# A one-layer mLSTM, attention and expert-lookup kernel: gathered rows consumed later, DRAM fetches moved forward, one more PSUM bank for U

## The chip, the cores and the metric

The kernel runs on one core of a Trainium2 chip. The metric is the device time of the core in microseconds (us), the median of three runs. Below, PE is the tensor engine (PEld its weight loads), DVE the vector engine, ACT the scalar engine, POOL the general-purpose engine, and SP the engine that here only issues DMAs. Every engine executes its own instructions in the order in which the program has them; semaphores tie engines to each other.

## What is computed

One layer over 512 tokens of width 2048, all in float32: a mixer of two branches (a chunked mLSTM and a causal attention with forget gates), a cross attention to 256 memory rows, and a lookup feed-forward, each followed by a residual and a layer norm. The feed-forward is where most of the change lies:

```python
q = (x @ w_pq).reshape(B, S, PEER_HEADS, 2, PEER_DK // 2)
sc = jnp.einsum('bshpd,hpnd->bshpn', q, sub_keys)
top_s, top_i = lax.top_k(sc, PEER_TOPK)
...
g = jax.nn.softmax(best_s, -1)
...
u = expert_u[it]                                   # 128 rows of 2048 for each token
a = jnp.einsum('tkd,td->tk', u, xt)
hact = jax.nn.gelu(a, approximate=False) * gt
return jnp.einsum('tk,tkd->td', hact, expert_v[it])
```

Each token picks 128 of 16384 experts (8 heads, 16 each), takes the dot product of the token with each expert's row of U, a gelu times the gate, and the sum of the experts' rows of V with these weights.

## The kernel before

**Weights.** Every large product is made from two float32r parts of each operand (high and low), so a product is three matmuls: high by high, high by low, low by high. A weight tile of 128 x 1024 comes by DMA into `raw` (L148, on SP's queue), ACT casts it to `whi` (L134), and DVE subtracts to get `wlo` (L137). In the first half every eighth such subtraction is made by POOL instead (L136, `SHARE`). The rings that hold these tiles are small: two to six `whi` and `wlo` in all.

**Token blocks.** Block A is the first 128 tokens, block B the other 384. A runs ahead through the whole mixer and the top-k, so that its experts are known while B still computes. In order, the stages are: A's path and the memory's projections, with B's mLSTM heads woven in; the end of B's heads (`run(heads)`, L1043); B's branch product (`branch_ml`, whose left operand is the tiles H, written to DRAM by the heads and loaded back, one tile pair to a weight load); B's attention (`fox`), its merge, output product, norm, cross attention, norm; B's top-k. Small pieces of attention and norm are "ridden" between weight loads (`mid`, `ride`, L166 to L179).

**Two ways through the experts.** Blocks A (128 tokens) and 96 further tokens (64 and 32) take the gathered way, `gathered` (L851). For each of its 128 choices (for fewer tokens, the 128 partitions hold several choices of one token at once), POOL issues an indirect DMA that puts one row of U per partition into `rows` (L846; 128 x 2048, three buffers), and DVE multiplies it with the token's own row `xacc` and sums (L860). Then the same is done for V, with a multiply-add into `xacc` (L873). The function is a generator: each `next` requests one row tile and emits the work on it. `load_w` calls it at a fixed rate while B computes (258 steps to 315 weight loads for block A). A gather carries a dependency on the newest weight split (`after(i, last())`), which keeps the requests from running ahead.

The other 288 tokens take the dense way: all 128 x 128 experts are gone through by first key. For first key `c`, `stage_a(c)` makes U's product (16 slices of the width by 3 parts, 48 matmuls into one PSUM bank `pa`, of which there are two), ACT applies the gelu into `ga` (L1223) and the result goes to DRAM (`gad`). Meanwhile the gates are built as one-hot products (L1182 to L1195) and written to DRAM (`gd`). `stage_h(c)` fetches both back (`G` for four keys at a time, `gb` for one, both on SP's queue, L1232 and L1236), multiplies them on DVE (L1240) and splits the product into `hph` and `hpl`. `stage_o` multiplies these with V: blocks of J = 8 keys, and for each block four quarters `q` of the width, four weight loads each. `stage_h` is called for the block's keys as quarter 0 comes to them. U runs LOOK = 68 keys ahead of V, so 68 keys are done before V starts, and the rest is interleaved with V by `fill`. Of the gathers' 194 steps for the 96 tokens, EARLY = 44 are taken in the first part and the rest in V; in V they are tied to the newest split of `stage_h` (`cur[0] = paced[c]`).

**Order.** Within an engine, the order of instructions is not that of the source: a scheduler places them by a timeline that it simulates, under the dependencies, the buffers of each pool and the manual dependencies of `after`.

Of the kernel before, what the change touches and what calls it, by code (L numbers as in the profile page):

```python
# [10 lines left out]
F32 = mybir.dt.float32  # L11
# [5 lines left out]
ALU = mybir.AluOpType  # L17
# [29 lines left out]
def build(tc, I, out):  # L47
    nc = tc.nc
    with ExitStack() as ctx:
# [461 lines left out]
        def fox(R, fp, ft, hold):  # L511
# [3 lines left out]
            def keys(qd):  # L515
                def ev(s, b, ks=quads[qd]["k"]):
                    ks[s] = ft(n)
                    nc.vector.tensor_copy(ks[s], b[:, :n])  # L518
# [331 lines left out]

        def gathered(t, r0, n, i, last):  # L851

# [4 lines left out]
            dots = gat.tile([P, P], F32, tag="dots", bufs=2, name=nm("dots"))  # L857
            for k in range(n):
                rows = gather_rows("peer_u", ei, k, last)
                nc.vector.scalar_tensor_tensor(rows, rows, 1.0, xacc, op0=ALU.mult, op1=ALU.mult,  # L860
                                               accum_out=dots[:, k:k + 1])
                yield True

            al = gat.tile([P, 1], F32, tag="al", bufs=1, name=nm("al"))
            if n < P:
                nc.vector.memset(al, 0.0)
            nc.vector.memset(al[:n], ALPHA)
            nc.scalar.mul(xacc, xacc, al)
            nc.scalar.activation(dots[:, :n], dots[:, :n], AF.Gelu)
            nc.vector.tensor_mul(dots[:, :n], dots[:, :n], gg[:, :n])  # L870
            for k in range(n):
                rows = gather_rows("peer_v", ei, k, last)
                nc.vector.scalar_tensor_tensor(xacc, rows, dots[:, k:k + 1], xacc, op0=ALU.mult, op1=ALU.add)  # L873
                yield True
            if n < P:
# [175 lines left out]
        with tc.tile_pool(name="hb", bufs=1, reuse_waits="tile") as hp:  # L1051
            HB = []
# [103 lines left out]

        def a_bank():
            return BK["pool"].tile([P, 512], F32, tag="s2", bufs=2, name=nm("pa"))

        def o_bank(i=0):  # L1160
# [41 lines left out]

        LOOK = 68
        EARLY = 44
        GA_N = 3
        J = 8
        gas, hs, paced, gates = {}, {}, {}, [None]
# [20 lines left out]

        def stage_h(c):
            if c % 4 == 0:  # L1230
                gt = mn.tile([P, NDENSE // GB, 4, GB], F32, tag="G", bufs=2, name=nm("G"))
                nc.sync.dma_start(gt, gd[:, :, c:c + 4])  # L1232
                gates[0] = gt
            if c in spilled:
                ga = mn.tile([P, NDENSE], F32, tag="gb", bufs=2, name=nm("gb"))
                nc.sync.dma_start(ga, gad[c])  # L1236
            else:
                ga = gas.pop(c)
            gv = ga.rearrange("p (b t) -> p b t", t=GB)
            nc.vector.tensor_mul(gv, gv, gates[0][:, :, c % 4])  # L1240
# [4 lines left out]
        cur = [None]  # L1245
        jobs = chain(*(gathered(TB - 1, r0, n, 1 + i, lambda: cur[0]) for i, (r0, n) in enumerate(GATHERED)))
        NT = -(-NDENSE // P)
        lwd, xr = [], {}

        def stage_o(c0, q, fill):  # L1250
# [3 lines left out]
            for m in range(J // 2):  # L1254
                vh, vl, _ = load_pair(I["vq"][c0 // 2 + m, q])
                todo = []
                for j in range(2):
                    c = c0 + 2 * m + j
                    if q == 0:
                        stage_h(c)  # L1260
                        cur[0] = paced[c]
                    a, b = hs[c]
                    for s in range(4):
                        sl = slice(j * 512 + s * P, j * 512 + (s + 1) * P)
                        todo.append((banks[s][:, :NDENSE], vh[:, sl], vl[:, sl], a, b, c, True))
                products(todo, c0, c0 + J - 1)
                fill(q * (J // 2) + m)
            if last and q == 0:
# [27 lines left out]
        for a in range(ahead[0]):  # L1296
            stage_a(a)
            cur[0] = work["last"]
            while done * LOOK < a * EARLY:
# [91 lines left out]
```

## Time and profile before

| | |
|---|---|
| time, median of 3 runs | 5062.73 us (5058.62 to 5063.53) |
| time of the profiled execution | 5072.05 us |
| its span | 5070.3 us |
| DMA moved | 1420.97 MB, mean 280 GB/s |
| mean granted PE clock | 0.977 |
| gathers (L846) | 224 of U, 224 of V |
| multiply on a row of U (L860) | 2336 ns each, DVE |
| multiply-add on a row of V (L873) | 2399 ns each, DVE |
| high part of a weight tile (L134) | 1051 ns each, ACT |
| low part of a weight tile (L137) | 1271 ns each, DVE |
| low part on POOL (L136) | 2579 ns each |

Engine times are busy times. A row of a view that ends in `[3.44 <-DVE c L518]` says that the engine stood idle for 3.44 us before this instruction and that what it waited for was DVE's write of the tile `c` in line 518. A row of waits reads: the waiting engine, tile and line, what it waited for, and then the total in us, how often, and the longest. Matmuls are pipelined, so the duration of one is longer than the distance to the next. The chain of waits that ended last runs along PE through the products of V and U, then through the last norm, which POOL and DVE finish.

### The profile page before, as it was taken

The page shows a single profiled execution, that of the slowest core. Times are in us where ns is not written, and L with a number is a line of the kernel's source. Part 1 is how long each engine was busy: PE and PEld are TensorE (multiplying, and loading weights), DVE is VectorE, ACT ScalarE, POOL GpSimd, SP SyncE. Part 2 cuts the span into 40 slices and gives each one's busy share as a digit, 9 for nine tenths or more (in the row PEclk, how much of TensorE's full clock was granted, in tenths as well). Part 3 has the DMA queues.
Part 4 walks back from the last instruction along what each step waited for, and adds up shares of the span by engine and source line. Part 5 has one row for each costly group of instructions (what it writes and reads, how often), then busy time and mean ns, then how long its engine had stood idle before and what let it go on. Part 6 is the DMA issues. An engine that isn't in the chain of part 4 may idle for free. (4 is left out here: it accounts for less than half of the span.)

```text
span 5070.3 us, 74427 instructions
## 1 busy us (share of the span) xinstructions
PE 4789.3 (94%) x28401; PEld 4397.2 (87%) x28401; DVE 3728.7 (74%) x5387; ACT 2122.9 (42%) x3046; POOL 1270.4 (25%) x1039
## 2 busy tenths in 40 slices
PE   7999999999989999998899999999989999999997
PEld 6888777777779999887888879999989999999987
DVE  6676767666977777666776565898878788787875
ACT  6556666565423233333224324434444333433332
POOL 1122223121324433323332221321001222121210
PEclk8999999999999999999999999999999999999998
DMA  7788878777689988777885774677769889898983
GB/s 247 254 283 284 279 261 276 264 249 234 225 310 357 351 326 305 275 257 260 293 323 212 258 254 162 211 256 259 281 248 364 328 336 344 328 354 321 358 302 123
DMA packets 375415, 1420.97 MB, mean 280 GB/s; under 512 B 43341, under 2 KB 104397, under 8 KB 316017
## 3 DMA queue, kind: packets, MB, share of 16 engines
q1 hardware_dynamic: 263904, 827.14, 47.3%
q0 software_dynamic: 89408, 551.06, 28.7%
q10 hardware_dynamic: 21744, 38.02, 2.0%
q8 instruction: 222, 3.64, 0.3%
q14 instruction: 137, 1.11, 0.1%
HBM read 1343.32 MB, written 72.62 MB: 279 GB/s over the span
## 5 line engine op out<-in xcount | busy, mean ns | idle before, releaser
L134 ACT CAST whi<-raw 128x1024 fp32r<-128x1024 f32 x1472 | 1533.0, 1051 | 2145.8 <-PE mm L205 823.3
L137 DVE TENSOR_TENSOR wlo<-raw,whi 128x1024 fp32r<-128x1024 f32 x1352 | 1703.7, 1271 | 698.8 <-ACT whi L134 504.6
L873 DVE SCALAR_TENSOR_TENSOR xacc<-rows,dots,xacc 128x2048 f32<-128x2048 f32 x224 | 537.3, 2399 | 220.6 <-DMA rows<-in_peer_v,eid 218.8
L860 DVE SCALAR_TENSOR_TENSOR rows<-rows,xacc 128x2048 f32<-128x2048 f32 x224 | 522.9, 2336 | 97.7 <-DMA rows<-in_peer_u,eid 97.6
L846 POOL DMA_INDIRECT rows<-in_peer_v,eid x224 | 336.0, 1500 | 1010.8 <-DVE wlo L137 389.5
L205 PE MATMUL pa<-Ch,whi 128*128 128x288 f32 x2048 | 564.8, 300 | 14.4 <-ACT ga L1223 13.0
L846 POOL DMA_INDIRECT rows<-in_peer_u,eid x224 | 309.6, 1382 | 1037.1 <-DVE rows L860 320.4
L205 PE MATMUL po<-hph,whi 128*128 128x288 f32 x2048 | 533.6, 298 | 32.6 <-ACT hph L134 27.3
L205 PE MATMUL pa<-Cl,whi 128*128 128x288 f32 x2048 | 562.8, 299 | 0.0
L205 PE MATMUL po<-hpl,whi 128*128 128x288 f32 x2048 | 533.1, 297 | 6.1 <-DVE hpl L137 6.1
L136 POOL TENSOR_TENSOR wlo<-raw,whi 128x1024 fp32r<-128x1024 f32 x120 | 309.5, 2579 | 723.8 <-ACT whi L134 444.4
L205 PE MATMUL mm<-xh,whi 128*128 128x384 f32 x1280 | 441.3, 347 | 9.1 <-DVE c L518 5.9
L205 PE MATMUL mm<-xl,whi 128*128 128x384 f32 x1280 | 433.9, 340 | 0.0
L205 PEld LDWEIGHTS po<-hph,whi 128*128 128x128 f32 x2048 | 374.8, 190 | 39.6 <-ACT hph L134 30.6
L205 PEld LDWEIGHTS pa<-Ch,whi 128*128 128x128 f32 x2048 | 389.8, 190 | 18.3 <-ACT ga L1223 14.8
L205 PEld LDWEIGHTS pa<-Cl,whi 128*128 128x128 f32 x2048 | 389.9, 190 | 1.7 <-issue 1.7
L205 PEld LDWEIGHTS po<-hpl,whi 128*128 128x128 f32 x2048 | 375.3, 190 | 7.4 <-DVE hpl L137 7.4
L205 PE MATMUL po<-hph,wlo 128*128 128x288 f32 x2048 | 349.5, 298 | 6.0 <-DVE wlo L137 6.0
L205 PE MATMUL pa<-Ch,wlo 128*128 128x288 f32 x2048 | 323.0, 297 | 3.7 <-DVE wlo L137 3.7
L205 PEld LDWEIGHTS po<-hph,wlo 128*128 128x128 f32 x2048 | 301.5, 191 | 6.5 <-DVE wlo L137 6.5
L205 PEld LDWEIGHTS pa<-Ch,wlo 128*128 128x128 f32 x2048 | 289.8, 189 | 4.7 <-DVE wlo L137 3.9
L205 PE MATMUL mm<-xh,wlo 128*128 128x384 f32 x1280 | 258.5, 337 | 5.3 <-DVE wlo L137 5.3
(440 smaller groups left out, 8778.6 us busy)
## 6 DMA issues: line engine op xcount, KB each, us to landing
raw<-in_w_in SPq DMA_DIRECT2D x512, 512.0 KB
raw<-in_uT SPq DMA_DIRECT2D x256, 512.0 KB
raw<-in_vq SPq DMA_DIRECT2D x256, 512.0 KB
raw<-in_w_xkv SPq DMA_DIRECT2D x64, 512.0 KB
raw<-in_w_br_ml SPq DMA_DIRECT2D x64, 512.0 KB
raw<-in_w_br_fx SPq DMA_DIRECT2D x64, 512.0 KB
raw<-in_w_out SPq DMA_DIRECT2D x64, 512.0 KB
raw<-in_w_xq SPq DMA_DIRECT2D x64, 512.0 KB
```

Of the source, the lines that this page charges most:

```text
L134: nc.scalar.copy(hi, src)
L136: return nc.gpsimd.tensor_sub(lo, src, hi.bitcast(F32))
L137: return nc.vector.tensor_sub(lo, src, hi.bitcast(F32))
L205: nc.tensor.matmul(o, w if stat else x, x if stat else w, start=k == first and x is xh and not part, stop=k == last and part == 1)
L846: i = nc.gpsimd.indirect_dma_start(out=rows, out_offset=None, in_=I[table], in_offset=bass.IndirectOffsetOnAxis(ap=ei[:, k:k + 1], axis=0))
L860: nc.vector.scalar_tensor_tensor(rows, rows, 1.0, xacc, op0=ALU.mult, op1=ALU.mult, accum_out=dots[:, k:k + 1])
L873: nc.vector.scalar_tensor_tensor(xacc, rows, dots[:, k:k + 1], xacc, op0=ALU.mult, op1=ALU.add)
```

## The change

- `gathered` requests a row tile and keeps it; the multiply on it is emitted `lag` steps later: two for block A, one for the other 96 tokens. The multiply now has a dependency on the newest weight split too (before, only the gather had one). The requests for V start while the last rows of U are still held.
- In V, "the newest split" is that of the last loaded weight tile of V or U, no longer that of `stage_h`.
- `fetch(c)` is taken out of `stage_h`. A call for key `c` also fetches `c+1` and `c+2` if these come from DRAM; `gb` has four buffers instead of two.
- In quarter 3 of a block, `stage_h` is called for the keys of the next block, two after each weight load.
- `stage_a` takes its bank from `sm_bank`, which goes round three banks, two of which are those that it had.
- LOOK is 72 instead of 68.
- The first 8 weight loads of B's branch are emitted before the rest of B's heads is settled and their pools are closed; its `sg` tiles get a pool of their own. H is loaded two tile pairs to a weight load.
- `keys` in the attention copies its tiles out of PSUM on ACT instead of DVE.

```diff
             def keys(qd):
                 def ev(s, b, ks=quads[qd]["k"]):
                     ks[s] = ft(n)
-                    nc.vector.tensor_copy(ks[s], b[:, :n])
+                    nc.scalar.copy(ks[s], b[:, :n])
...
-        def gathered(t, r0, n, i, last):
+        def gathered(t, r0, n, i, last, lag):
...
-            for k in range(n):
-                rows = gather_rows("peer_u", ei, k, last)
-                nc.vector.scalar_tensor_tensor(rows, rows, 1.0, xacc, op0=ALU.mult, op1=ALU.mult,
-                                               accum_out=dots[:, k:k + 1])
+            held = []
+
+            def use():
+                s, rows = held.pop(0)
+                k = s % n
+                if s == n:
...
+                    nc.scalar.mul(xacc, xacc, al)
+                    nc.scalar.activation(dots[:, :n], dots[:, :n], AF.Gelu)
+                    nc.vector.tensor_mul(dots[:, :n], dots[:, :n], gg[:, :n])
+                if s < n:
+                    after(nc.vector.scalar_tensor_tensor(rows, rows, 1.0, xacc, op0=ALU.mult, op1=ALU.mult,
+                                                         accum_out=dots[:, k:k + 1]), last())
+                else:
+                    after(nc.vector.scalar_tensor_tensor(xacc, rows, dots[:, k:k + 1], xacc,
+                                                         op0=ALU.mult, op1=ALU.add), last())
+
+            for s in range(2 * n):
+                if len(held) == lag:
+                    use()
+                held.append((s, gather_rows("peer_v" if s >= n else "peer_u", ei, s % n, last)))
                 yield True
...
-            for k in range(n):
-                rows = gather_rows("peer_v", ei, k, last)
-                nc.vector.scalar_tensor_tensor(xacc, rows, dots[:, k:k + 1], xacc, op0=ALU.mult, op1=ALU.add)
-                yield True
+            while held:
+                use()
...
-        work.update(jobs=gathered(0, 0, P, 0, lambda: work["last"]), rate=258 / 315)
+        work.update(jobs=gathered(0, 0, P, 0, lambda: work["last"], 2), rate=258 / 315)
         run(heads)
+        sgp = ctx.enter_context(ExitStack())
+        sg = sgp.enter_context(tc.tile_pool(name="sg", bufs=1, side="right", reuse_waits="tile"))
+        HB = []
+        branch = branch_ml(B, HB, lambda: sg.tile([P, B.n], F32, tag="sg", bufs=9, name=nm("sg")))
+        for _ in range(8):
+            next(branch)
         settle()
...
-            mid(*[load_h] * 16)
-            run(branch_ml(B, HB, lambda: hp.tile([P, B.n], F32, tag="sg", bufs=9, name=nm("sg"))))
+            mid(*[lambda: (load_h(), load_h())] * 8)
+            run(branch)
+        sgp.close()
...
-        LOOK = 68
+        LOOK = 72
...
-            bank = a_bank()[:, :NDENSE]
+            bank = sm_bank()[:, :NDENSE]
...
-        def stage_h(c):
+        fetched = {}
+
+        def fetch(c):
+
             if c % 4 == 0:
                 gt = mn.tile([P, NDENSE // GB, 4, GB], F32, tag="G", bufs=2, name=nm("G"))
                 nc.sync.dma_start(gt, gd[:, :, c:c + 4])
                 gates[0] = gt
             if c in spilled:
-                ga = mn.tile([P, NDENSE], F32, tag="gb", bufs=2, name=nm("gb"))
+                ga = mn.tile([P, NDENSE], F32, tag="gb", bufs=4, name=nm("gb"))
                 nc.sync.dma_start(ga, gad[c])
             else:
                 ga = gas.pop(c)
+            fetched[c] = ga, gates[0]
+
+        def stage_h(c):
+            for f in range(c, min(c + 3, NC_)):
+                if f in fetched:
+                    continue
+                if f != c and f not in spilled:
+                    break
+                fetch(f)
+            ga, gt = fetched[c]
...
-            paced[c] = split(a, b, ga)
+            split(a, b, ga)
...
-        jobs = chain(*(gathered(TB - 1, r0, n, 1 + i, lambda: cur[0]) for i, (r0, n) in enumerate(GATHERED)))
+        jobs = chain(*(gathered(TB - 1, r0, n, 1 + i, lambda: work["last"], 1) for i, (r0, n) in enumerate(GATHERED)))
...
-                vh, vl, _ = load_pair(I["vq"][c0 // 2 + m, q])
+                vh, vl, work["last"] = load_pair(I["vq"][c0 // 2 + m, q])
...
-                    if q == 0:
+                    if c not in hs:
                         stage_h(c)
-                        cur[0] = paced[c]
...
                 products(todo, c0, c0 + J - 1)
+                if q == 3 and not last:
+                    for c in (c0 + J + 2 * m, c0 + J + 2 * m + 1):
+                        stage_h(c)
                 fill(q * (J // 2) + m)
```

More of the change, by code (lines that the diff above doesn't have):

```diff
@@ L857, in gathered @@
             dots = gat.tile([P, P], F32, tag="dots", bufs=2, name=nm("dots"))
-            for k in range(n):
-                rows = gather_rows("peer_u", ei, k, last)
-                nc.vector.scalar_tensor_tensor(rows, rows, 1.0, xacc, op0=ALU.mult, op1=ALU.mult,
-                                               accum_out=dots[:, k:k + 1])
-                yield True
[L864 to L870, printed above, removed]
-            for k in range(n):
-                rows = gather_rows("peer_v", ei, k, last)
-                nc.vector.scalar_tensor_tensor(xacc, rows, dots[:, k:k + 1], xacc, op0=ALU.mult, op1=ALU.add)
-                yield True
+            held = []
[3 more added lines that the diff above has]
+                if s == n:
+                    al = gat.tile([P, 1], F32, tag="al", bufs=1, name=nm("al"))
+                    if n < P:
+                        nc.vector.memset(al, 0.0)
+                    nc.vector.memset(al[:n], ALPHA)
+                    nc.scalar.mul(xacc, xacc, al)
[11 more added lines that the diff above has]
+                held.append((s, gather_rows("peer_v" if s >= n else "peer_u", ei, s % n, last)))
+                yield True
+            while held:
+                use()
             if n < P:
@@ L1051, in build @@
         with tc.tile_pool(name="hb", bufs=1, reuse_waits="tile") as hp:
-            HB = []
             def load_h():
@@ L1155, in build @@
         work["share"] = 0
-        def a_bank():
-            return BK["pool"].tile([P, 512], F32, tag="s2", bufs=2, name=nm("pa"))
         def o_bank(i=0):
@@ L1206, in build @@
         J = 8
-        gas, hs, paced, gates = {}, {}, {}, [None]
+        gas, hs, gates = {}, {}, [None]
         rings[:] = [W, E]
         def stage_a(c):
-            bank = a_bank()[:, :NDENSE]
+            bank = sm_bank()[:, :NDENSE]
             for kt in range(2):
@@ L1238, in stage_h @@
                 ga = gas.pop(c)
+            fetched[c] = ga, gates[0]
[7 more added lines that the diff above has]
+            ga, gt = fetched[c]
             gv = ga.rearrange("p (b t) -> p b t", t=GB)
-            nc.vector.tensor_mul(gv, gv, gates[0][:, :, c % 4])
+            nc.vector.tensor_mul(gv, gv, gt[:, :, c % 4])
             a, b = pair(mn, "hp", [P, NDENSE], 2 * J + 2)
-            paced[c] = split(a, b, ga)
+            split(a, b, ga)
             hs[c] = (a, b)
-        cur = [None]
-        jobs = chain(*(gathered(TB - 1, r0, n, 1 + i, lambda: cur[0]) for i, (r0, n) in enumerate(GATHERED)))
+        jobs = chain(*(gathered(TB - 1, r0, n, 1 + i, lambda: work["last"], 1) for i, (r0, n) in enumerate(GATHERED)))
         NT = -(-NDENSE // P)
@@ L1297, in build @@
             stage_a(a)
-            cur[0] = work["last"]
             while done * LOOK < a * EARLY:
```

## The prediction

> **What bounds the kernel now.** I read the page's totals first, then a table of stretches, then who waits for whom inside the stretches that the change touches, and last single rows of the timeline. The profiled execution has a span of 5070.3 us and a time of 5072.05 us; the median of the runs is 5062.73. Terms below are in the profiled execution's own time, and I take the sum off the median, 9.3 us lower.
>
> ```profile
> span 5070.3 us, 74427 instructions
> ...
> PE 4789.3 (94%) x28401; PEld 4397.2 (87%) x28401; DVE 3728.7 (74%) x5387; ACT 2122.9 (42%) x3046; POOL 1270.4 (25%) x1039
> ```
>
> The tensor engine (PE) sets the end: it is busy 94% of the span, and no other engine is over 74%. No matmul is added or removed, so the change can only win what PE loses. Where it loses, the table of stretches shows (start:end, length, then busy time of PE, PEld, DVE, ACT, POOL, granted clock, share of the DMA engines, GB/s):
>
> ```profile
> 0.00:1300.00 1300.00, 1231.41 (x5977) 1013.50 (x5978) 908.78 (x1375) 782.83 (x1068) 296.37 (x286) 0.98 0.78 263
> ...
> 1400.00:1500.00 100.00, 82.88 (x389) 70.77 (x388) 75.72 (x108) 29.10 (x41) 30.25 (x25) 0.91 0.82 303
> 1500.00:2050.00 550.00, 548.64 (x3085) 529.38 (x3085) 408.73 (x475) 175.32 (x233) 214.48 (x162) 1.00 0.90 334
> 2050.00:2450.00 400.00, 353.09 (x1823) 320.64 (x1822) 251.45 (x281) 117.08 (x190) 122.85 (x102) 0.95 0.73 259
> 2450.00:3050.00 600.00, 571.63 (x2803) 502.39 (x2802) 400.07 (x400) 190.53 (x260) 186.63 (x163) 0.98 0.73 267
> ...
> 3250.00:3750.00 500.00, 471.25 (x3514) 466.19 (x3513) 439.17 (x922) 205.76 (x435) 90.51 (x66) 0.98 0.76 272
> 3750.00:3800.00 50.00, 30.57 (x202) 28.50 (x201) 29.67 (x76) 15.63 (x59) 1.70 (x2) 0.83 0.61 226
> 3800.00:4900.00 1100.00, 1080.01 (x8017) 1069.23 (x8016) 892.32 (x981) 430.26 (x529) 232.54 (x157) 0.99 0.92 343
> 4900.00:5000.00 100.00, 88.19 (x614) 83.74 (x614) 55.76 (x82) 36.24 (x46) 4.50 (x5) 0.93 0.61 201
> ```
>
> Idle PE time is length less busy time: 17.1 us where block B's heads give way to its branch (1400:1500), 46.9 in the attention and merge of B (2050:2450), 28.8 where top-k, U and the gates are built (3250:3750), 19.4 at the start of V (3750:3800), 20.0 over all of V (3800:4900) and 11.8 at its last block (4900:5000). The clock falls in the same stretches, so some of the busy time there is slow as well. These two rows of one form (4 matmuls of 384 columns) say how: after an idle 1.49 us they took 0.97 us, after 3.12 us they took 1.65.
>
> ```profile
> 2396.75 0.97 PE L205 MATMUL mm<-Ah,whi 128*128 128x384 f32 x4 [1.49 <-ACT Ah L141]
> ...
> 2440.26 1.65 PE L205 MATMUL mm<-Al,whi 128*128 128x384 f32 x4 [3.12 <-DVE Al L142]
> ```
>
> **Gathered rows used two steps later (A).** DVE runs in order, and today it stands still until a gathered row has landed. Total waits of DVE for rows, in 1400:1500, 1500:2050, 2050:2450 and 2450:3050:
>
> ```profile
> DVE rows L860 <- DMA rows<-in_peer_u,eid: 11.8, 6, 5.4
> ...
> DVE rows L860 <- DMA rows<-in_peer_u,eid: 44.5, 22, 4.2
> ...
> DVE xacc L873 <- DMA rows<-in_peer_v,eid: 116.4, 34, 8.5
> ...
> DVE xacc L873 <- DMA rows<-in_peer_v,eid: 90.0, 34, 7.7
> ```
>
> Such a wait reaches PE like this: DVE loses 3.69 us on a row, multiplies it for 2.35, only then copies four key tiles out of PSUM, and PE has stood 3.44 us for that copy.
>
> ```profile
> 2201.41 2.35 DVE L873 SCALAR_TENSOR_TENSOR xacc<-rows,dots,xacc 128x2048 f32<-128x2048 f32 x1 [3.69 <-DMA rows<-in_peer_v,eid]
> ...
> 2203.74 1.94 DVE L518 COPY c<-mm 128x384 f32<-128x384 f32 x4
> ...
> 2204.35 0.44 PE L205 MATMUL mm<-xh,whi 128*128 128x384 f32 x1 [3.44 <-DVE c L518]
> ```
>
> How long does a row take? Counted from the first of each, these are the 127th gather and the 127th multiply: 7.6 us from issue to use, with DVE waiting.
>
> ```profile
> 2034.19 1.00 POOL L846 DMA_INDIRECT rows<-in_peer_u,eid  x1 [0.76 <-DVE wlo L137]
> ...
> 2041.79 2.29 DVE L860 SCALAR_TENSOR_TENSOR rows<-rows,xacc 128x2048 f32<-128x2048 f32 x1 [3.00 <-DMA rows<-in_peer_u,eid]
> ```
>
> A step comes every 315/258 weight loads. A load carries 24 matmuls of 0.178 us (550 us by 3085), 4.3 us, so a step is 5.2 us and two steps 10.4: longer than 7.6. The built order of both programs agrees. In the stretch 2050:2450 (gathers 128 to 184) there lie 0 or 1 weight splits of DVE between the split that a gather waits for and its multiply in 37 of 51 cases before, 2 or more in 49 of 57 after. So I expect nearly all of the 116.4 us to go. What PE gets of it is bounded by PE's own waits in 2050:2450:
>
> ```profile
> PE mm L205 <- DVE Al L142: 11.6, 6, 3.6
> PE sm L590 <- DVE fst L576: 8.7, 2, 5.0
> ...
> PE mm L205 <- DVE c L518: 5.9, 2, 3.4
> PE sm L590 <- DVE fpt L597: 5.8, 2, 5.1
> PE mm L205 <- DVE wlo L137: 2.9, 3, 1.6
> PE mm L205 <- POOL wlo L136: 2.5, 1, 2.5
> ```
>
> Without the key copies those behind DVE are 11.6+8.7+5.8+2.9 = 29.0. I take two thirds, 19, since 0:1300, which the change leaves almost alone, has 5.3% idle anyway, and that much of 400 us (21) should remain here. In 2450:3050 idle is 4.7%, below that floor: 0, though DVE waits 90 us there.
>
> **Key copies on ACT (L518).** Sixteen copies for B, 0.49 us each in the row above, and sixteen small ones for A. ACT is busy 117 of 400 us, and other evictions of that shape sit on it already; DVE loses 8 us of work. The 5.9 us of PE waits bound the gain; 0 is the other end if ACT has them late instead. I take 4.
>
> The clock in 2050:2450 costs at most 0.05 of 353 us, 18; in proportion to idle time won (23 of 46.9) that is 9. Sum of the stretch: 19+4+9 = 32, between 8 and 60. [...]
>
> **Eight loads of the branch moved ahead of the heads' end.** Waits of PE in 1400:1500:
>
> ```profile
> PE sm L488 <- DVE st L480: 6.7, 1, 6.7
> PE mm L205 <- DVE wlo L137: 5.3, 3, 2.4
> PE sm L488 <- DVE o L483: 4.2, 2, 2.4
> ```
>
> In the built order the 12 transposes of the last head (L488), which stood in one row, now have some 170 branch matmuls between and ahead of them: the DVE chain of the norm (6.7+4.2) gets cover. The wlo waits lie beside row waits (11.8); I take half. The clock costs at most 0.09 of 83 us, 7.5; I take 6. Against it: the H tiles are now loaded two to a weight load over 8 loads instead of one over 16. A load then moves 0.52 MB of weights, 0.39 of H and 0.82 rows of 1.05 MB, 1.77 MB in 4.3 us, or 412 GB/s. At the 334 GB/s of 1500:2050 it takes 5.3 us, 8 us late over eight loads; at no cost if the raw buffers carry it. I take 3. Sum 10.9+2.6+6-3 = 16, between 0 and 24.
>
> **U in three banks, LOOK 72.** In 3250:3750 PE waits for the bank that the gelu empties:
>
> ```profile
> PE pa L205 <- ACT ga L1223: 13.0, 8, 3.3
> ...
> PE pa L205 <- DVE wlo L137: 3.7, 1, 3.7
> ```
>
> A third bank gives each gelu one more key (48 matmuls, 6.5 us at 0.135, 1080 us by 8017) of patience, against a longest wait of 3.3; I take 9 of 13.0, as the bank is shared with the scores. From wlo 3, from the clock (0.02 of 471) 4: 16, between 3 and 25. [...]
>
> LOOK moves 4 keys of U (26 us of PE) ahead of V's start. Today the gates' last piece runs alone, one group of four matmuls per round of DVE (0.60 us from start to start, then 1.10), and then PE waits for the first gates to go out to DRAM and come back:
>
> ```profile
> 3764.46 0.68 DVE L1182 TENSOR_TENSOR o<-iota,i1T 128x512 f32<-128x512 f32 x1
> 3765.06 1.10 DVE L1188 TENSOR_SCALAR o<-iota,i0T,gT 128x128 f32<-128x128 f32 x4
> ...
> PE po L205 <- ACT hph L134: 14.4, 1, 14.4
> ```
>
> In the built order 51 matmuls of the gates stand alone at the end before, 24 after: 27 less, or 6.75 rounds of 1.7 us, 11 us; part of that is PE's own work, so I take 8. The 14.4 stay in my sum, because the first load of gates still follows the last store. Between 0 and 25.
>
> **Fetch three keys ahead, next block's split at q = 3 (B).** In 3800:4900, then 4900:5000:
>
> ```profile
> DVE gb L1240 <- DMA gb<-gad: 42.7, 18, 9.1
> ...
> PE po L205 <- ACT hph L134: 6.8, 5, 2.1
> ...
> PE po L205 <- ACT hph L134: 6.1, 1, 6.1
> PE po L205 <- DVE hpl L137: 4.2, 2, 2.2
> ```
>
> The fetches (144 KB, 126 as before; gates as before) go on SP's queue up to two keys earlier, ahead of weight loads; four gb buffers hold them. The split of the next block is then done before the block starts, and the last block's no longer stands behind the finish of the last gathered tokens. Of 6.8 I take 5, of 6.1+4.2 I take 8, of the last stretch's clock (0.07 of 88, 6) 3: 16, between 5 and 28. Behind a multiply that now waits for the newest split stand the next split and the accumulations, but the split that it waits for is already ahead of it on DVE; I price this wait at 0, and it is the seed of the slow rival.
>
> Sum: 32+16+16+8+16 = 88. Not all of it stays: what DVE no longer delays, ACT or a weight ring may. I keep 0.85, 75 us: 5062.7-75 = 4988.
>
> **Rivals.**
> Clock stays (5006). The gaps shrink, but enough remain for the clock to fall back: the 9+6+4+3 = 22 of clock are not won, 0.85 of them 18. For it: the clock is 0.98 even in 0:1300.
> DVE's waits are not PE's limit (5030). For it: in 1500:2050 DVE waits 44.5 us for rows and PE is busy 548.6 of 550. If in 2050:2450 ACT's splits or the one weight ring of the merge come late in DVE's stead, only the U, gate and V terms (16+8+16 = 40, 0.85 of it 34) remain.
> It doesn't do what it says (5063): the scheduler puts multiplies back beside their gathers. The built order speaks against it.
> Slower (5105). A gather still needs the buffer of the row three steps back, which is now freed a step later. Every eighth weight split runs on POOL, behind that gather. 1500:3050 has 7711 matmuls, 321 loads, 40 such splits; at the 2.5 us that PE once waited for one, that costs 100. The U, gate and V terms still give 34, and I leave 24 of the other 41: 5062.7+100-34-24 = 5105. It decides from the point where PE's waits on POOL splits exceed 75 us. Against it: 2.5 us in one single wait is all that 2050:2450 shows today.
> More (4935): the upper ends, the 14.4 at V's start hidden too.
>
> **How the numbers follow.** Chances: forecast 0.45, clock stays 0.15, DVE not the limit 0.20, nothing 0.06, slower 0.10, more 0.04. The upper ends of the bounds sum to 60+24+25+25+28 = 162, of which I take 0.8 (130) for the low end, 4932; the lower ends sum to 8+0+3+0+5 = 16, which gives the high end, 5047. That range leaves out the slower case and no change. What can be told from no change is 0.2%, 10 us. Faster 0.83, same 0.06, slower 0.11.
>
> **What would show it.** DVE's waits for rows in B's attention near 20 us instead of 116.4; PE's waits for c L518 gone; the 6.7 before L488 gone; PE's waits for ga under 4; the last block's hph wait gone; a wait near 14 us still at V's start. I am wrong if PE's idle time in B's attention stays near 47 us while those DVE waits are gone, or if waits on POOL splits grow.

## The result, and the profile after

| | before | after |
|---|---|---|
| median | 5063.13 us (5058.62 to 5066.74, 4 runs) | 4951.45 us (4946.76 to 4957.46, 4 runs) |
| profiled execution | 5072.05 us | 4954.55 us |
| its span | 5070.3 us | 4952.8 us |
| mean granted clock | 0.977 | 0.985 |

The ratio is 0.9781, with a 95% interval of 0.9764 to 0.9797: the change wins 112 us where 75 were forecast; the time lies between the 4932 and the 5047 of the prediction. The first lines of the page of the changed kernel:

```profile
span 4952.8 us, 74559 instructions
...
PE 4747.2 (96%) x28401; PEld 4370.2 (88%) x28401; DVE 3713.1 (75%) x5355; ACT 2123.3 (43%) x3078; POOL 1416.2 (29%) x1039
```

The number of matmuls is the same. PE's busy time fell by 42 us (the mean granted clock rose from 0.977 to 0.985), its idle time by the other 75.

Where did it come from? Fixed stretches of time no longer hold the same work, so I cut both traces at the same events: the first and last matmul of block B's branch on H, the first and last of the merge's output on A, the first of U and the first of V. The table of stretches between them for the kernel before (start:end, length, busy time of PE, PEld, DVE, ACT, POOL, granted clock, DMA share, GB/s):

```profile
1420.00:1531.00 111.00, 93.88 (x473) 85.18 (x472) 81.49 (x114) 34.61 (x51) 34.59 (x26) 0.91 0.80 293
1531.00:1731.00 200.00, 200.00 (x1156) 200.00 (x1155) 143.88 (x137) 55.91 (x62) 83.65 (x58) 1.00 0.94 353
1731.00:2387.00 656.00, 625.69 (x3383) 578.75 (x3381) 463.94 (x571) 210.87 (x323) 222.14 (x178) 0.98 0.80 290
2387.00:2559.00 172.00, 149.87 (x780) 144.10 (x779) 114.72 (x104) 46.05 (x61) 70.91 (x66) 0.93 0.84 309
2559.00:3211.00 652.00, 623.18 (x3161) 552.65 (x3160) 403.62 (x553) 223.99 (x319) 167.78 (x145) 0.98 0.64 229
3211.00:3783.00 572.00, 523.82 (x3898) 516.75 (x3899) 497.16 (x1121) 235.50 (x508) 104.53 (x83) 0.97 0.73 261
3783.00:5039.00 1256.00, 1223.88 (x9028) 1207.71 (x9028) 981.00 (x1115) 480.61 (x592) 238.75 (x163) 0.99 0.86 320
```

The same of the changed kernel:

```profile
1420.00:1525.00 105.00, 91.91 (x474) 84.92 (x473) 73.06 (x105) 31.26 (x44) 37.78 (x27) 0.93 0.80 297
1525.00:1737.00 212.00, 203.77 (x1155) 201.03 (x1154) 159.25 (x148) 59.95 (x69) 102.01 (x59) 0.99 0.90 342
1737.00:2350.00 613.00, 612.71 (x3379) 571.62 (x3379) 446.33 (x550) 217.52 (x338) 269.81 (x177) 1.00 0.84 309
2350.00:2509.00 159.00, 144.11 (x780) 137.93 (x780) 117.45 (x105) 46.06 (x61) 73.44 (x67) 0.97 0.89 334
2509.00:3147.00 638.00, 619.30 (x3163) 551.79 (x3162) 404.17 (x551) 224.08 (x318) 202.56 (x145) 0.98 0.63 234
3147.00:3716.00 569.00, 540.29 (x4089) 537.29 (x4089) 511.74 (x1134) 243.96 (x520) 117.74 (x86) 0.97 0.77 276
3716.00:4922.00 1206.00, 1190.97 (x8837) 1177.40 (x8838) 963.59 (x1105) 461.60 (x581) 269.15 (x160) 0.99 0.88 327
```

Row by row: heads' end and branch +6; B's attention -43; merge -13; from there to U -14; U -3, though it now holds four keys more (191 matmuls, 26 us), so -29; V -50, of which 26 were moved, so -24. In the attention PE's idle time went from 30.3 us to 0.3 and its clock to 1.00.

Who waits for whom in attention and merge (before 1731:2559, after 1737:2509; a row gives the waiting engine, tile and line, the releaser, total us, times, longest). DVE's waits for rows before:

```profile
DVE xacc L873 <- DMA rows<-in_peer_v,eid: 125.6, 39, 8.5
...
DVE rows L860 <- DMA rows<-in_peer_u,eid: 25.4, 14, 3.2
```

After, the two largest of PE's waits:

```profile
PE mm L205 <- DVE Al L142: 7.0, 6, 3.1
PE mm L205 <- ACT Ah L141: 6.6, 8, 2.7
```

And after, DVE's waits for rows and one that is new:

```profile
DVE xacc L877 <- DMA rows<-in_peer_v,eid: 15.2, 14, 2.9
...
DVE xacc L877 <- POOL wlo L136: 12.6, 5, 3.3
...
DVE rows L874 <- DMA rows<-in_peer_u,eid: 12.5, 8, 3.6
```

DVE's wait for rows fell from 151 us to 28. Gone from PE's list, but for 0.2 us of `fpt`, are its waits for `fst`, `fpt`, `c`, for DVE's `wlo` and for POOL's `wlo`. New is a wait of DVE for a split made on POOL: the multiply's tie, when the newest split is one of the eighth that POOL makes. The timeline of DVE there shows the new order, the multiply right behind a split, with no wait of its own (start, length, engine, line, tiles, idle before it):

```profile
2073.98 1.23 DVE L137 TENSOR_TENSOR wlo<-raw,whi 128x1024 fp32r<-128x1024 f32 x1 [0.89 <-ACT whi L134]
2075.24 2.35 DVE L877 SCALAR_TENSOR_TENSOR xacc<-rows,dots,xacc 128x2048 f32<-128x2048 f32 x1
```

The heads' end behaved otherwise. PE's largest waits there after (1420:1737):

```profile
PE mm L205 <- ACT whi L134: 10.7, 2, 8.1
PE mm L205 <- DVE wlo L137: 3.9, 3, 2.0
```

ACT's timeline around the longest of them:

```profile
1494.66 0.58 ACT L1041 ACTIVATE ht<-sm,c_norm_w 128x384 f32<-128x384 f32 x1 [7.62 <-DMA htd<-ht]
...
1495.54 1.04 ACT L134 CAST whi<-raw 128x1024 fp32r<-128x1024 f32 x1
```

The waits for L488 (6.7 and 4.2) are covered, as forecast. But the last head's tiles leave through one buffer `ht`, ACT stands 7.6 us until the store before has left it, and the cast of the next weight tile stands behind that on ACT.

### The profile page after: what moved, and what is told of

It reads as the page before. It is cut to its first block, busy times and chain, and to the rows that moved or that the text cites. A ratio compares the mean times of both kernels' runs of the same rounds, so it can differ in the third digit from the quotient of the medians.

```text
span 4952.8 us, 74559 instructions
## 1 busy us (share of the span) xinstructions
PE 4747.2 (96%) x28401; PEld 4370.2 (88%) x28401; DVE 3713.1 (75%) x5355; ACT 2123.3 (43%) x3078; POOL 1416.2 (29%) x1039
## 5 line engine op out<-in xcount | busy, mean ns | idle before, releaser
L846 POOL DMA_INDIRECT rows<-in_peer_v,eid x224 | 435.3, 1943 | 836.1 <-DVE wlo L137 457.8
L846 POOL DMA_INDIRECT rows<-in_peer_u,eid x224 | 363.2, 1622 | 939.0 <-DVE wlo L137 370.4
L877 DVE SCALAR_TENSOR_TENSOR xacc<-rows,dots,xacc 128x2048 f32<-128x2048 f32 x224 | 530.3, 2367 | 69.9 <-POOL wlo L136 38.5
L205 PE MATMUL po<-hph,whi 128*128 128x288 f32 x2048 | 552.6, 297 | 18.4 <-ACT hph L134 14.4
L205 PE MATMUL sm<-Ch,whi 128*128 128x288 f32 x2048 | 561.0, 298 | 4.7 <-ACT whi L134 2.9
L205 PE MATMUL sm<-Cl,whi 128*128 128x288 f32 x2048 | 558.3, 297 | 0.0
L205 PEld LDWEIGHTS sm<-Ch,whi 128*128 128x128 f32 x2048 | 387.5, 189 | 6.9 <-ACT whi L134 3.1
L205 PEld LDWEIGHTS sm<-Cl,whi 128*128 128x128 f32 x2048 | 387.4, 189 | 0.8 <-issue 0.8
L205 PE MATMUL po<-hph,wlo 128*128 128x288 f32 x2048 | 329.9, 296 | 5.4 <-DVE wlo L137 5.3
L205 PE MATMUL sm<-Ch,wlo 128*128 128x288 f32 x2048 | 320.5, 297 | 4.1 <-DVE wlo L137 4.1
L205 PEld LDWEIGHTS sm<-Ch,wlo 128*128 128x128 f32 x2048 | 287.7, 189 | 5.6 <-DVE wlo L137 5.5
L205 PEld LDWEIGHTS mm<-xh,whi 128*128 128x128 f32 x1280 | 242.1, 189 | 24.9 <-ACT whi L134 12.8
```

The costliest lines, as they stand in the source:

```text
L205: nc.tensor.matmul(o, w if stat else x, x if stat else w, start=k == first and x is xh and not part, stop=k == last and part == 1)
L846: i = nc.gpsimd.indirect_dma_start(out=rows, out_offset=None, in_=I[table], in_offset=bass.IndirectOffsetOnAxis(ap=ei[:, k:k + 1], axis=0))
L877: after(nc.vector.scalar_tensor_tensor(xacc, rows, dots[:, k:k + 1], xacc, op0=ALU.mult, op1=ALU.add), last())
```

## The experiments

Each ran beside the kernel before on the same chip. The three groups of experiments (`a1` to `a4`, `a5` to `a8`, and `b2` to `c_best`) were on different chips. The kernel before had a median of 5063.13 us beside the changed kernel, and of 5071.01, 5077.59 and 5069.59 us in the three groups; so kernels of different groups are compared by their ratios and by the lengths of single stages.

**What makes the rows pay: the lag, or the tie?** `a1_no_lag` puts `gathered` back as it was and leaves the rest of the change.

```diff
...
-            for s in range(2 * n):
-                if len(held) == lag:
-                    use()
-                held.append((s, gather_rows("peer_v" if s >= n else "peer_u", ei, s % n, last)))
+            for k in range(n):
+                rows = gather_rows("peer_u", ei, k, last)
+                nc.vector.scalar_tensor_tensor(rows, rows, 1.0, xacc, op0=ALU.mult, op1=ALU.mult,
+                                               accum_out=dots[:, k:k + 1])
                 yield True
...
```

> The changed kernel with the gathered rows used at once again (no lag, no dependency of the multiply on a split); all other edits stay. Theory 1 (DVE's waits for rows hold PE in B's attention, merge and cross attention, where the changed kernel gained 43, 13 and 14 us): about 60 us come back, 5010 us, ratio to the kernel before 0.990, and DVE's waits for rows are near 300 us again. Rival (the key copies on ACT and the reordering around them made the gain in the attention, the row waits are hidden): 4950 to 4965 us, ratio 0.978 to 0.981, although the row waits return.

Measured: 5066.65 us, ratio 0.9993 (0.9979 to 1.0007), no change from the kernel before. Neither theory expected so much: without this part nearly the whole gain is gone.

`a2_no_tie` keeps the lag and takes the multiply's dependency on the newest split away, for U's rows as for V's.

```diff
...
-                    after(nc.vector.scalar_tensor_tensor(xacc, rows, dots[:, k:k + 1], xacc,
-                                                         op0=ALU.mult, op1=ALU.add), last())
+                    nc.vector.scalar_tensor_tensor(xacc, rows, dots[:, k:k + 1], xacc,
+                                                   op0=ALU.mult, op1=ALU.add)
```

> The changed kernel with the lag kept, but without the new dependency of the multiply on the newest split. Theory 1 with the lag alone as its cause: within 6 us of the changed kernel (4945 to 4957), or a little faster, since DVE's 38 us of waits of the multiply for a split made by POOL go. Rival (the tie does the work: without it the scheduler moves the multiplies back to their gathers): the row waits return to over 150 us and the time goes up by 30 us or more, 4980.

Measured: 5059.17 us, ratio 0.9978 (0.9962 to 0.9995). The lag in the source, without the tie, is worth next to nothing. The reason stands in the built order. For gathers 128 to 184 (the attention), I counted DVE's weight splits between the split that a gather waits for and its multiply: at most one in 37 of 51 cases before, in 8 of 57 after; in `a1_no_lag` and in `a2_no_tie` alike at most one in 38 of 51. The scheduler, free to place the multiply, puts it back beside its gather. In the trace DVE's waits for rows are then what they were, attention and merge (1727:2565) of `a2_no_tie`:

```profile
DVE xacc L877 <- DMA rows<-in_peer_v,eid: 127.6, 40, 9.5
DVE rows L874 <- DMA rows<-in_peer_u,eid: 44.9, 17, 6.7
```

No run has the tie without the lag. By the code the multiply would then be tied to the split that its own gather waits for, and could again stand right behind it; that is argued.

`b2_lag_alone` is the kernel before with the lag and the tie and nothing else (the rows' code as in the diff of the change; in V the tie is to the newest split of `stage_h`, as for the gathers).

> The kernel before, with one part of the change alone: the rows are used two steps (96 tokens: one step) behind their request, and the multiply is tied to the newest split (in V to that of stage_h, as the gathers were). Theory 1: this part is worth the same alone as in the changed kernel, where taking either half of it away cost all but some 4 of 112 us in U's stretch and before; in its stages that was fox 43 to 52, merge 7 to 13, the way to U 8 to 12 and U 27 to 30, some 95 us: a ratio of 0.979 to 0.984. Rival 2: part of the 95 is owed to the other edits (three banks and 72 keys in U, keys on ACT): then only fox, merge and top-k win, 55 to 70 us, a ratio of 0.986 to 0.990, and U's stage stays near 572 us.

Measured: 4971.88 us, ratio 0.9813 (0.9788 to 0.9838), theory 1: 95 us of the kernel before's 5069.59 (0.0187 of it), from this part alone. By stages, against the kernel before: attention 656.4 to 613.1, merge 171.9 to 163.0, the way to U 652.0 to 639.1, U 571.9 to 549.5, V 1256.5 to 1244.6. The row of the attention, busy without a gap:

```profile
1725.00:2338.00 613.00, 613.00 (x3384) 572.21 (x3383) 456.71 (x570) 211.46 (x323) 267.83 (x178) 1.00 0.84 310
```

**The key copies.** `a3_keys_dve`:

```diff
-                    nc.scalar.copy(ks[s], b[:, :n])
+                    nc.vector.tensor_copy(ks[s], b[:, :n])
```

> The changed kernel with the key copies back on DVE. Theory 1 (with the row waits gone, DVE has the copies in time): 0 to 3 us slower, 4951 to 4954, and no wait of PE for the copies (line 518) over 1 us. Rival (the copies on ACT won the 5.9 us that PE waited for them, as the prediction's 4 has it): 4 to 8 us slower, 4955 to 4960, with such waits.

Measured: 4945.33 us, ratio 0.976 (0.9735 to 0.9786). The attention takes 613.1 us, as with the copies on ACT, and no wait for `c` L518 came back. With the copies on ACT, but the rows used as before, `a1_no_lag` takes 658.2 us there. The copies were late only because rows made DVE late.

**The branch's early loads.** `a4_no_early_branch`:

```diff
-        for _ in range(8):
-            next(branch)
...
-            mid(*[lambda: (load_h(), load_h())] * 8)
+            mid(*[load_h] * 16)
```

> The changed kernel with B's branch begun after the heads are settled and one H pair to a weight load, as before. The two traces say that the early loads gained 6 us up to the first H matmul and that 12 us were lost again up to the last one. Theory 2 (the edit loses as a whole: ACT waits 7.6 us for the single ht buffer with weight casts behind it, and H comes too fast): 3 to 10 us faster, 4941 to 4948. Rival (the prediction's 16 us: the edit gains, and something else lost the 12 us): 4960 to 4967.

Measured: 4942.66 us, ratio 0.9759 (0.9732 to 0.9785). The interval overlaps that of the changed kernel, so the ratio alone does not settle it; the stages speak more clearly. The branch takes 199.8 to 200.5 us in all four kernels without the early loads and 211.0 to 223.5 in the ten with them, while its first matmul on H starts at 1524.3 to 1536.3 without and at 1510.9 to 1527.6 with them. In the means, what comes 9 us earlier takes 14 longer. PE's waits there (1420:1731) are those of before again:

```profile
PE sm L488 <- DVE st L480: 6.7, 1, 6.7
PE sm L488 <- DVE o L483: 4.2, 2, 2.3
```

`a8_ht3` asks whether the one `ht` buffer is the cause: three of them, in the pool of the `sg` tiles.

```diff
-                t = mb.tile([P, B.n], F32, tag="ht", bufs=1, name=nm("ht"))
+                t = htp[0].tile([P, B.n], F32, tag="ht", bufs=htp[1], name=nm("ht"))
...
+            htp = [mb, 1]
...
+        htp[:] = [sg, 3]
```

> The changed kernel with three ht buffers, in the sg pool, for the heads' tiles that are written once the branch has begun. Theory 2 (one ht buffer: ACT waits 7.6 us for its write to DRAM with two weight casts behind, and PE 8.1 us for those): 6 to 12 us faster, 4939 to 4945, and the wait of 8.1 us is gone. Rival (ACT and DVE then wait for the H tiles from DRAM instead, which are late for lack of DMA rate): 4948 to 4954.

Measured: 4950.11 us, ratio 0.9752 (0.9736 to 0.9768); the last matmul on H ends at 1734.4, against 1736.7. The wait for `whi` is gone, but the tiles of H, which have to go to DRAM and come back, take its place (1400:1737):

```profile
PE mm L205 <- ACT Hh L141: 8.5, 5, 4.2
PE mm L205 <- DVE Hl L142: 4.0, 2, 3.5
```

So the buffer made one wait, not the loss: what started early had to wait for H. Why H is late then, no run shows.

**The third bank.** `a5_two_banks`:

```diff
-            bank = sm_bank()[:, :NDENSE]
+            bank = BK["pool"].tile([P, 512], F32, tag="s2", bufs=2, name=nm("pa"))[:, :NDENSE]
```

> The changed kernel with U's products in two PSUM banks again. Theory 3 (PE's 13.0 us of waits for the gelu before are a matter of banks): 6 to 12 us slower, 4957 to 4963, with PE waiting over 5 us in total for ga. Rival (the gelu was late because DVE and ACT stood behind row waits; the bank does nothing): 4949 to 4954 and waits for ga under 4 us.

Measured: 4951.9 us, ratio 0.976 (0.9744 to 0.9777): no loss. U takes 570.3 us against 569.2. PE waits longer for the gelu in U's stretch, and still nothing is lost at the end:

```profile
PE pa L205 <- ACT ga L1237: 6.8, 5, 3.9
```

The same wait in the changed kernel:

```profile
PE sm L205 <- ACT ga L1237: 1.6, 4, 0.5
```

Two other runs show where the 13.0 us of before went. `b2_lag_alone`, below, uses the rows later and has two banks as before (3140:3689):

```profile
PE pa L205 <- ACT ga L1235: 3.6, 5, 2.1
```

`a1_no_lag` has three banks and uses the rows as before. Its wait for the gelu is 1.5 us, but that for the gates' one-hot tiles, which DVE makes, is 26.2 us against 11.8 before (3206:3802):

```profile
PE po L1193 <- DVE o L1191: 26.2, 14, 7.1
```

Its U, less the 26 us of four more keys, takes 570 us, where the kernel before took 572. With the rows as before, the third bank moved PE's wait to something else that comes from DVE; the later use of the rows took most of it away.

**Keys of U ahead of V.** `a6_look68`:

```diff
-        LOOK = 72
+        LOOK = 68
```

> The changed kernel with LOOK = 68. Theory 4 (4 keys of U fill the gates' last piece, which DVE paces): 6 to 12 us slower, 4957 to 4963. Rival (the fill is worth nothing, because PE waits for the first gates from DRAM anyway): 4949 to 4954.

Measured: 4967.77 us, ratio 0.9793 (0.9771 to 0.9816). Against the two kernels of the same chip whose edits cost nothing (`a5_two_banks` 4951.9, `a8_ht3` 4950.1) that is 16 to 18 us; U and V together take 1783.7 us against their 1768.9 and 1773.3, 10 to 15 (and 9 against the 1774.8 of the changed kernel). PE waits more for the gates' one-hot tiles, 16.0 us, against 4.5 in the changed kernel:

```profile
PE po L1204 <- DVE o L1202: 16.0, 19, 2.7
```

**Fetch ahead and early split.** `a7_no_fetch_ahead` takes out both:

```diff
-                ga = mn.tile([P, NDENSE], F32, tag="gb", bufs=4, name=nm("gb"))
+                ga = mn.tile([P, NDENSE], F32, tag="gb", bufs=2, name=nm("gb"))
...
-            for f in range(c, min(c + 3, NC_)):
+            for f in range(c, c + 1):
...
-                if q == 3 and not last:
+                if False:
```

> The changed kernel with the fetches of V back at their key (two gb buffers) and the split of a block's keys at its own quarter 0. Theory 5 (fetch and early split are what V gained): 12 to 22 us slower, 4963 to 4973, with DVE's waits for gb near 50 us and a wait for hph of about 6 us at the last block. Rival (V gained because the gathers are paced by the newest weight split): 4948 to 4956.

Measured: 5016.62 us, ratio 0.9893 (0.9872 to 0.9914): some 65 us slower, several times the whole term of the forecast. V takes 1261.7 us instead of 1205.6. Which half is it? `b3_split_early_only` has the first two edits of that diff, `b4_fetch_only` the last alone.

> The changed kernel without the fetch ahead: a call of stage_h fetches its own key alone and gb has two buffers, but the next block's splits still come in quarter 3. Taking out both cost 65 us, 56 of them in V. Theory 1: the loss came from the splits at quarter 0, with PE waiting for hph at the block starts (58.8 us in 15 waits there); with the splits early, a late fetch is covered by a quarter of a block: 4945 to 4965, a ratio of 0.974 to 0.979. Rival 2: the fetch itself holds up DVE and with it everything behind it (DVE waits for gb 55.6 us there, 10.1 in the changed kernel): 4985 to 5015, a ratio of 0.983 to 0.989.

> The changed kernel with the fetch three keys ahead and four gb buffers, but the block's splits come at its own quarter 0, none in quarter 3. Theory 1 (the early split does the work): PE still waits 40 to 60 us for hph at the block starts: 5000 to 5020, a ratio of 0.987 to 0.990. Rival 2 (the fetch does it): DVE's waits for gb fall to some 10 us, and PE's waits for hph below 20: 4950 to 4970, a ratio of 0.976 to 0.981.

Measured: `b3_split_early_only` 5011.38 us, ratio 0.988 (0.9857 to 0.9902), V 1264.0; `b4_fetch_only` 4954.49 us, ratio 0.9773 (0.9745 to 0.9802), V 1205.9. The fetch ahead, with its two more buffers, does it all; the early split does nothing, and rival 2 holds for both. Theory 1 named the right wait (PE for `hph`) and the wrong cause. The waits in V of `b3_split_early_only` (3718:4982):

```profile
PE po L205 <- ACT hph L134: 63.0, 15, 14.5
DVE gb L1267 <- DMA gb<-gad: 59.9, 31, 6.6
DVE xacc L877 <- DMA rows<-in_peer_v,eid: 49.5, 33, 5.7
...
DVE rows L874 <- DMA rows<-in_peer_u,eid: 27.6, 22, 3.2
```

and in V of `b4_fetch_only` (3718:4924):

```profile
DVE rows L874 <- DMA rows<-in_peer_u,eid: 18.4, 7, 5.9
...
PE po L205 <- ACT hph L134: 14.6, 1, 14.6
...
DVE gb L1267 <- DMA gb<-gad: 10.5, 10, 2.0
```

The first of those 15 waits, 14.5 us, is the one at V's start. One of the others in the timelines of `b3_split_early_only`, DVE first:

```profile
4207.21 2.35 DVE L877 SCALAR_TENSOR_TENSOR xacc<-rows,dots,xacc 128x2048 f32<-128x2048 f32 x1 [2.46 <-DMA rows<-in_peer_v,eid]
4209.48 0.45 DVE L1267 TENSOR_TENSOR gb<-gb,G 128x288 f32<-128x288 f32 x1
```

then ACT, which cuts the high part of the product:

```profile
4209.96 0.43 ACT L134 CAST hph<-gb 128x288 fp32r<-128x288 f32 x1 [8.77 <-DVE gb L1267]
```

and PE, which needs that part:

```profile
4210.44 1.57 PE L205 MATMUL po<-hph,whi 128*128 128x288 f32 x5 [7.11 <-ACT hph L134]
```

Here it is a row that is late: DVE waits 2.46 us for it, multiplies for 2.35, and only then makes the product from which the split is cut. It is not so in all of them: around the 14 waits after V's start (each wait and the 6 us ahead of it) DVE stood 10.7 us for rows and 9.3 us for `gb`. In the built order the multiplies of gathers 300 to 447 (those in V) stand, in the mean, 3.8 weight splits behind the one that their gather waits for, in the changed kernel 5.7. So without the fetch ahead the rows are used sooner as well, and how much of the 58 us is the rows' and how much the fetch's own lateness, these two runs do not divide. `b2_lag_alone` helps: it has no fetch ahead either, but ties V's rows to `stage_h`'s split, and its V, less the 26 us of the four keys, takes 1219 us. `a1_no_lag` and `a2_no_tie`, which have the fetch ahead but use the rows beside their gathers, take 1211.2 and 1213.3 us in V, 17 to 19 less than the 1230 of the kernel before without the four keys. So the fetch ahead saves some 13 to 19 us where the rows are used as before or with the old tie, and 58 where the tie is the new one. That last step is argued, since U's banks, the number of keys and the pacing of the gathers differ too.

**All together.** `c_best` is the changed kernel with the early loads of the branch left out, the key copies on DVE and LOOK 78.

> The changed kernel with its branch loads left where they were before, the key copies on DVE, and 78 keys of U ahead of V instead of 72. Theory 1: the gains add up: some 9 us from the branch, 0 to 6 from the copies, and 10 to 14 from the keys, which cover the 14.4 us wait at V's start: 4920 to 4940, a ratio of 0.971 to 0.975. Rival 2: V, which then has fewer keys of U to fill it, loses what its start wins, and the branch and the copies share one gain: 4940 to 4952, a ratio of 0.975 to 0.978.

Measured: 4947.81 us, ratio 0.9758 (0.9734 to 0.9782), rival 2. Against `b4_fetch_only` on the same chip, which is as good as the changed kernel, that is 6.7 us; U and V together take 1765.7 us instead of 1775.7. Its interval overlaps the changed kernel's, so it is not shown to be better. The wait at V's start shrank, but did not go:

```profile
PE po L205 <- ACT hph L134: 10.3, 1, 10.3
```

## Why the prediction was right, and where it was not

What bounds the kernel (PE's idle time, and the lower clock in the same stretches) held: 75 us of the 117 us between the two spans are idle time of PE, 42 its busy time, at a mean granted clock of 0.985 instead of 0.977. Of the terms, that for the rows was far too small and that for LOOK somewhat; fetch and split came out near its size, though not by the split; the copies and the third bank held nothing, and the branch had the wrong sign:

| term | forecast | measured |
|---|---|---|
| rows used later, attention and merge (with 4 for key copies) | 32 | 56; the copies 0 |
| rows used later, on the way to U | 0 | 14 (13 by `b2_lag_alone`) |
| rows used later, in U | none | 22 by `b2_lag_alone` |
| branch loads ahead | 16 | -5 to -9 |
| third bank (9), splits and clock in U (7) | 16 | bank 0 |
| rows used later, in V | none | 12 by `b2_lag_alone` |
| LOOK 72 | 8 | 9 to 18 |
| fetch ahead and early split | 16 | fetch ahead 13 to 19 (argued), early split 0; V won 24 in all, with the rows |

So the total came out as near as it did partly by luck. The rows with the copies, priced at 32, were worth some 95, and all the other terms together, priced at 56, brought some 17: errors of opposite sign.

**Rows used later.** The mechanism was right, the size was not. The failed step is "I take two thirds, 19, since 0:1300 ... has 5.3% idle anyway". That stretch is no floor for another one: the attention's idle time went to 0.3 of 613 us. Idle time of attention and merge fell by 37 (30.3+22.1 before, 0.3+14.9 after) where 19+4 were taken, and the clock gave 19 (busy time 775.6 to 756.8, at 1.00 and 0.97 instead of 0.98 and 0.93) instead of 9. By the same floor 2450:3050 was put at 0; it gave 14. U was not in this term at all, though DVE waited 38.7 us for rows there before (3211:3783):

```profile
DVE rows L860 <- DMA rows<-in_peer_u,eid: 38.7, 21, 4.9
```

**The tie ("I price this wait at 0").** As a cost that was nearly right: over the whole changed kernel DVE's multiplies wait 38.5 us in 11 times and 14.3 in 5 for POOL's splits, but PE is idle for 0.3 us in the attention and no longer waits for a POOL split in any of B's stages. What the prediction missed is that without the tie the lag does next to nothing. I had read its effect in the built order and put it down to the lag.

**Branch loads ahead.** The cover for L488 came (10.9 of PE's waits gone), and the failed step is the 3 set against it, which took the rate of the DMAs alone as the limit. H's way through DRAM, and the one `ht` buffer on that way, had no term.

**Third bank.** The failed step is "I take 9 of 13.0". `a5_two_banks` halves the wait of before without a third bank (6.8 us), and the rest costs nothing that the runs can tell: the ratio is 0.976 without the third bank beside 0.9781 with it. `b2_lag_alone` brings the wait down to 3.6 us. That the gelu was the releaser was no proof that the bank was the limit.

**LOOK, fetch and split.** LOOK's reason held: the gates' last piece overlaps with U, and the 14.4 us at V's start stayed, as said. The 24 us in V lie within the 5 to 28 given, but some 12 of them came with the rows, for which V had no term. The 8 for the last block and the 5 for `hph` were credited to the split at quarter 3, and that edit alone is worth nothing.

**The factor 0.85** pointed the wrong way, since other stages gained too.

**Rivals.** The clock did not stay (0.98 in the attention before, 1.00 after). DVE's waits were PE's limit there. The slower case needed more than 75 us of PE waiting for POOL's splits in B's stages: PE has no such wait there any more, and the 2.5 us of before are gone. That the scheduler puts the multiplies back was a rival too; it is what `a1_no_lag` and `a2_no_tie` show, and the tie prevented it in the changed kernel.

Do the parts add up? From ratios and stages: 95 (lag with tie) + 9 to 18 (LOOK) + 13 (fetch) - 5 to 9 (branch) = 108 to 121, against 112. But they need each other: with everything except the lag and the tie, only 4 us remain of the median (`a1_no_lag`). The stages of single executions are less sure than that: the one of `a1_no_lag` that was profiled took 5046.0 us, where the median is 5066.65.

## What to carry to other kernels

When an engine works in order and one of its operands comes by a slow transfer, ask in the built order how far the use stands behind the request; where a scheduler places instructions, only a dependency keeps that distance, and reordering the source does not. The gain of such a step is bounded by the idle time of the bounding engine in every stage where the waits occur, with the clock there (19 us of busy time beside 37 of idle time in attention and merge), and not by the idle share of some other stage: it went to 0.3 us in the attention, though 14.9 us stayed in the merge. An edit that starts work earlier must be followed to where its operands come from: the branch started 9 us earlier and took 14 longer.

## What the runs showed of the hardware that was not expected

The clock did not follow the length of a single gap. Four matmuls of 384 columns took 1.65 us after a gap of 1.99 us in `c_best`, and 0.96 after one of 3.13 us in `a6_look68`, in the same stage (the merge). The first, in PE's timeline:

```profile
2381.95 1.65 PE L205 MATMUL mm<-Ah,whi 128*128 128x384 f32 x4 [1.99 <-ACT Ah L141]
```

The second:

```profile
2365.20 0.96 PE L205 MATMUL mm<-Al,whi 128*128 128x384 f32 x4 [3.13 <-DVE Al L142]
```

Short windows around the two rows show the granted clock beside PE's work (start:end, length, busy time of PE, granted clock, DMA share, GB/s). In `c_best`:

```profile
2378.54:2381.96 3.42, 1.43 (x10) 1.00 0.88 302
2381.96:2385.37 3.41, 3.41 (x11) 0.50 0.11 41
```

In `a6_look68`:

```profile
2362.88:2366.30 3.42, 1.10 (x6) 1.00 1.00 381
2366.30:2369.71 3.41, 3.41 (x13) 0.50 1.04 408
```

In both, a window at clock 0.50 comes behind one in which PE was busy for 1.43 and 1.10 of 3.42 us. The matmuls behind the gap of 1.99 us stood in the window at 0.50; those behind the gap of 3.13 us were done at 2366.16, just before theirs began at 2366.30.

The traces of the kernels before and after show the same. From 1400 us on, their stretches at clock 0.50 last 3.41 us or two to five times that, but for the last one of each. With the span cut into windows of that length along these stretches, PE was busy for at most 1.70 us in each of the 43 windows at full clock behind which one at 0.50 came, and for at least 1.68 us in each of the 1981 behind which another at full clock came. Before 1400 us some windows do not fit: at 1016.82 us in the kernel before, PE was busy for 3.21 us, and a window at 0.50 came all the same. The clock's part in attention and merge was 19 us. In the sums of the two profiled executions, 75 us of idle time went together with 42 us of busy time, more than half as much again.
